# Gate and up projection in seven block products for each pair, value products of two heads on both column halves

## The chip, the cores and the metric

The kernel runs on one core of a Trainium2 chip. Its time is in device microseconds, the median of several executions. One more execution is recorded by the hardware profiler; the rows below are from it. Engines: TensorE (PE) multiplies, with its weight loads listed apart as PEld; VectorE (DVE), ScalarE (ACT) and GpSimd (POOL) do elementwise work; SyncE (SP) issues the DMAs.

## The reference

512 tokens of width 1024 pass a first block (a state-space scan, spatial gating, a mixture of experts) and then two layers of a second block. A layer has three attention branches, an output projection, and a dense feed-forward with 2816 hidden features. What the change touches, cut to its core:

```python
# neighbourhood attention, 8 heads of 64, per query block
sc = einsum('bnqhd,banchd->bhnqac', qb, kb) * scale + bias
p = softmax(where(col_valid, sc, -inf))
o = einsum('bhnqac,banchd->bnqhd', p, vb)
...
# differential attention, 4 heads, two score maps each
o = a1 - lam * a2
...
# dense feed-forward
gu = einsum('bsd,df->bsf', x, w_ffn_in[l])
hidden = silu(gu[..., :D_FF]) * gu[..., D_FF:]
ffn = einsum('bsf,fd->bsd', hidden, w_ffn_out[l])
x = layer_norm(DN_ALPHA * x + ffn, ln2_g[l], ln2_b[l])
```

## The kernel before

Every large product is done in three matmuls. An f32 operand `a` is split into a rounded part `ah` (a cast on ScalarE, L106) and the rest `al = a - ah` (a subtraction on VectorE, L107); `mm3` (L115 to L117) adds `ah*bh`, `al*bh` and `ah*bl` in PSUM. Weights come from memory in chunks of 128 x 1024 (`load_w`), are split into `whi` and `wlo` (three buffers each) and used.

A layer runs `mla`, `diff`, `na` (the three attention branches), `w_out2` (output projection, layer norm, transposition of the tokens into `xTh` and `xTl`) and `ffn`. In `ffn`, the hidden features come in 22 pairs of blocks of 128: `pg` is the gate block, `pu` the up block, each 8 chunks of the width times three matmuls of 512 tokens. The first two pairs work on column halves of 256 tokens, so that they can start when half of the tokens are there. Then come silu (L1688), the product (L1689) and the split of the hidden block into `hh` and `hl` (L1692, L1693), which all stay in SBUF. The down projection goes over the output in two halves `q`, over the 22 hidden blocks in 11 steps `i` of two, and over four token tiles `t`, each with its own PSUM tile.

In `na`, for a pair of heads `m` and two query blocks `i`, scores are 64 rows deep (L115 to L117 with `nqh`, `nkh`, heads on rows 0-63 and 64-127). After the softmax and a transposition (L1618) the value products (L1625) write both heads to PSUM rows 0-63, at different columns. In `diff`, two score maps of 64 rows each are computed one after the other.

PSUM has four tiles tagged `mm` and four tagged `aux`. The code is written in the order of the mathematics, but a scheduler places the instructions of each engine by its own estimate of time, so the order on an engine is not the written one. SyncE's loads go in order as buffers come free.

Of the kernel before, what the change touches and what calls it, by code (L numbers as in the profile page):

```python
# [17 lines left out]
NT = 4  # L18
# [19 lines left out]
class Net:  # L38
# [51 lines left out]
    def mm(self):  # L90
        return self.ps.tile([128, 512], F32, name="mm", tag="mm", bufs=4)
# [1365 lines left out]
    def diff(self, l):  # L1457
# [102 lines left out]
    def na(self, l):  # L1560
# [30 lines left out]
        for j in range(4):  # L1591
# [2 lines left out]
            gw = self.gate_w(0, l, 1)  # L1594
            for np_ in range(2):
                po = self.aux()
                for m in range(2):
                    r = slice(64 * m, 64 * m + 64)
                    hc = slice((2 * j + m) * 64, (2 * j + m + 1) * 64)
                    bt = at.tile([128, 512], F32, name="nb", tag="nb", bufs=4)  # L1600
                    nc.sync.dma_start(bt, self.a["na_bias"][l, j, np_, m])
                    ps = self.mm()
                    for i in range(2):
                        n = 2 * np_ + i
                        qs, ks = slice(n * 128, (n + 1) * 128), slice(kb[n], kb[n] + 256)
                        self.mm3(ps[:, i * 256:(i + 1) * 256], qh[r, qs], ql[r, qs], kh[r, ks], kl[r, ks], True, True)
# [14 lines left out]
                    for i in range(2):  # L1621
                        n = 2 * np_ + i
                        T, i0 = (VP, kb[n] // 128) if kb[n] % 128 == 0 else (VSH, kb[n] // 128)
                        for ii in range(2):
                            nc.tensor.matmul(po[0:64, m * 256 + i * 128:m * 256 + i * 128 + 128], T[:, i0 + ii, hc], PT[:, (2 * i + ii) * 128:(2 * i + ii + 1) * 128], start=ii == 0, stop=ii == 1)  # L1625
                    if np_ == 0 and m == 1 and j < 3:
                        nxt = prep(j + 1)
                src = [po[0:64, m * 256:(m + 1) * 256].rearrange("p (g r c) -> p g r c", g=4, r=8) for m in range(2)]
                dst = lambda x, m: perm(x[j][64 * m:64 * m + 64])[:, 4 * np_:4 * np_ + 4]
                for m in range(2):  # L1630
                    nc.scalar.copy(dst(oh, m), src[m])
                for m in range(2):
                    V.tensor_tensor(dst(ol, m), src[m], dst(oh, m).bitcast(F32), OP.subtract)
            self.gate(0, l, gw)
            for i in range(ng - 1):
                self.gate(0, l, self.gate_w(0, l))
# [11 lines left out]
    def w_out2(self, l):  # L1648
# [12 lines left out]
        for t in range(NT):  # L1661
# [6 lines left out]
                V.scalar_tensor_tensor(self.x[t][:, c], self.x[t][:, c], math.sqrt(2.0), p, op0=OP.mult, op1=OP.add)  # L1668
            self.layer_norm(self.x[t], LN_EPS, lg, lb)
            if t == 0:  # L1670
                self.new_xT()
            self.xT_block(self.x[t], t)
            self.dump("xa%d_%d" % (l, t), self.x[t])
        wo.release()

    def ffn(self, l):
        nc = self.nc
        V = nc.vector
        hp = self.pool("hid")
        tp = self.pool("hidt")  # L1680
        hh, hl = [], []
        for b in range(22):
            pg, pu = self.mm(), self.mm()
            outs = lambda p: [(p, slice(0, 256)), (p, slice(256, 512))] if b < 2 else [(p, ALL)]
            self.feat(self.a["w_f1"][l, b], self.xh, self.xl, outs(pg))
            self.feat(self.a["w_f1"][l, 22 + b], self.xh, self.xl, outs(pu))
            s = tp.tile([128, 512], F32, name="fs", tag="fs", bufs=3)
            nc.scalar.activation(s, pg, AF.Silu)  # L1688
            V.tensor_tensor(s, s, pu, OP.mult)  # L1689
            h = hp.tile([128, 512], F32R, name="hh%d" % b)  # L1690
            lo = hp.tile([128, 512], F32R, name="hl%d" % b)
            nc.scalar.copy(h, s)  # L1692
            V.tensor_tensor(lo, s, h.bitcast(F32), OP.subtract)  # L1693
            hh.append(h)
            hl.append(lo)
        lg, lb = self.bcast2(tp, "ln2_g", l), self.bcast2(tp, "ln2_b", l)

        ahead = 4
        st = [tp.tile([128, 2, 6], F32, name="fst%d" % t) for t in range(NT)]
        for q in range(2):  # L1700
            c = slice(q * 512, (q + 1) * 512)
            ps = [self.mm() for _ in range(NT)]
            last = 11 if q == 0 else 11 - ahead

            def mms(t, i, w):
                ts = slice(t * 128, (t + 1) * 128)
                for kk in range(2):
                    k, o = 2 * i + kk, slice(kk * 512, (kk + 1) * 512)
                    self.mm3(ps[t], hh[k][:, ts], hl[k][:, ts], w[0][:, o], w[1][:, o], k == 0, k == 21)

            for i in range(last):
                w = self.load_split(self.a["w_f2"][l, q, i], 1024)
                for t in range(NT):
                    mms(t, i, w)
            ws = []
            for i in range(last, 11):
                to = [tp.tile([128, 1024], F32R, name="fw" + n, tag="fw" + n, bufs=ahead - 3) for n in "hl"] if i < last + ahead - 3 else ()
                ws.append(self.split(self.load_w(self.a["w_f2"][l, q, i], 1024), 1024, *to))
# [177 lines left out]
```

## Time and profile before

| | us |
|---|---|
| median of 3 runs | 3253.01 (3251.31 to 3254.45) |
| the profiled execution | 3246.04 |
| its span | 3244.3 |
| PE busy | 3098.5 (96%) |
| VectorE busy | 2020.1 (62%) |
| ScalarE busy | 1453.4 (45%) |

The span runs from the first to the last instruction on the core; the profiled execution's time is 1.7 us more. Busy times of PE are sums in which overlapping matmuls count once. The first block fills the span to about 1302 us, the two layers the rest; layer 1's gate and up projection is the stretch from 2864 to 3112 us.

### The profile page before, as it was taken

The numbers are of one execution on the slowest core, as the hardware profiler recorded it, in microseconds if no ns is written. First come the engines' busy times: TensorE is split into PE (matmuls) and PEld (weight loads), VectorE is DVE, ScalarE is ACT, GpSimd is POOL, SyncE is SP. The second block draws the span as 40 slices with busy tenths as digits, with TensorE's granted clock in tenths as the row PEclk, the third lists the DMA queues.
The fourth block names the chain that finished last, engine by engine and source line by source line (L and its number), as shares of the span: only waits on it lengthen the run. The fifth ranks groups of instructions, "written<-read, shape, count | busy, mean of one in ns | idle before, by whom it ended". The sixth has DMA issues, their size and how long they took to land. (4 is left out here: it accounts for less than half of the span.)

```text
span 3244.3 us, 39811 instructions
## 1 busy us (share of the span) xinstructions
PE 3098.5 (96%) x14802; PEld 2447.2 (75%) x14802; DVE 2020.1 (62%) x3374; ACT 1453.4 (45%) x2455; POOL 378.1 (12%) x295
## 2 busy tenths in 40 slices
PE   7999999969999997899999999999999999999998
PEld 4887777746665654788777788888888777888887
DVE  7778765569888888676655653324675655653324
ACT  6544432347767775364544422221464534422221
POOL 1454200132121123000110000000000110000000
PEclk9999999979999999999999999999999999999999
DMA  5112245569999995112233322222312143422222
GB/s 194 53 43 76 93 152 180 181 255 405 342 349 353 366 355 199 67 57 75 69 119 119 113 89 98 91 98 88 107 59 80 59 146 98 135 67 97 91 98 78
DMA packets 140763, 469.82 MB, mean 145 GB/s; under 512 B 16268, under 2 KB 20364, under 8 KB 140568
## 3 DMA queue, kind: packets, MB, share of 16 engines
q1 hardware_dynamic: 139416, 463.08, 41.2%
q0 software_dynamic: 1152, 4.19, 0.3%
q8 instruction: 116, 1.90, 0.2%
q14 instruction: 79, 0.65, 0.1%
HBM read 456.71 MB, written 10.50 MB: 144 GB/s over the span
## 5 line engine op out<-in xcount | busy, mean ns | idle before, releaser
L107 DVE TENSOR_TENSOR wlo<-raw,whi 128x1024 fp32r<-128x1024 f32 (+4 forms) x384 | 434.0, 1133 | 515.7 <-ACT whi L106 514.5
L115 PE MATMUL mm<-xTh,whi 128*128 128x512 f32 (+2 forms) x1648 | 633.3, 385 | 6.1 <-ACT P L1233 2.6
L106 ACT CAST whi<-raw 128x1024 fp32r<-128x1024 f32 (+4 forms) x384 | 363.2, 948 | 603.0 <-PE mm L116 246.1
L116 PE MATMUL mm<-xTh,wlo 128*128 128x512 f32 (+2 forms) x1648 | 629.7, 383 | 0.0
L117 PE MATMUL mm<-xTl,whi 128*128 128x512 f32 (+2 forms) x1648 | 628.0, 382 | 0.7 <-POOL xTl L260 0.3
L115 PEld LDWEIGHTS mm<-xTh,whi 128*128 128x128 f32 (+1 forms) x1648 | 310.1, 188 | 75.7 <-ACT P L1233 4.2
L117 PEld LDWEIGHTS mm<-xTl,whi 128*128 128x128 f32 (+1 forms) x1648 | 309.7, 188 | 66.6 <-DVE xTl L260 1.5
L116 PEld LDWEIGHTS mm<-xTh,wlo 128*128 128x128 f32 (+1 forms) x1648 | 310.4, 188 | 62.9 <-issue 0.9
L115 PE MATMUL mm<-whi,xTh 128*128 128x512 f32 (+1 forms) x536 | 206.2, 386 | 2.5 <-DVE zt L555 2.1
L116 PE MATMUL mm<-whi,xTl 128*128 128x512 f32 (+1 forms) x536 | 205.8, 384 | 0.0
L117 PE MATMUL mm<-wlo,xTh 128*128 128x512 f32 (+1 forms) x536 | 203.0, 384 | 0.0
L1006 PE MATMUL mm<-wlo,XS 128*128 128x512 f32 x336 | 114.4, 412 | 18.3 <-DVE wlo L945 13.4
L116 PE MATMUL mm<-whi,hl 128*128 128x512 f32 x336 | 130.8, 389 | 0.0
L115 PE MATMUL mm<-whi,hh 128*128 128x512 f32 x336 | 130.4, 389 | 0.0
L117 PE MATMUL mm<-wlo,hh 128*128 128x512 f32 x336 | 129.7, 389 | 0.0
L1397 POOL TENSOR_TENSOR ql<-q,qh 128x512 fp32r<-128x512 f32 x16 | 20.6, 1290 | 885.0 <-ACT qh L1396 885.0
L115 PEld LDWEIGHTS mm<-whi,xTh 128*128 128x128 f32 x536 | 100.7, 188 | 23.0 <-DVE zt L555 2.5
L117 PEld LDWEIGHTS mm<-wlo,xTh 128*128 128x128 f32 x536 | 100.5, 188 | 19.6
L116 PEld LDWEIGHTS mm<-whi,xTl 128*128 128x128 f32 x536 | 100.7, 188 | 19.3
L945 DVE TENSOR_TENSOR wlo<-mraw,whi 128x1024 fp32r<-128x1024 f32 x82 | 108.7, 1341 | 8.9 <-ACT whi L943 8.6
L1005 PE MATMUL mm<-whi,XS 128*128 128x512 f32 x336 | 111.3, 405 | 1.6 <-ACT whi L943 1.6
L1689 DVE TENSOR_TENSOR fs<-fs,mm 128x512 f32<-128x512 f32 x44 | 30.3, 688 | 128.7 <-PE mm L117 128.7
(721 smaller groups left out, 6356.1 us busy)
## 6 DMA issues: line engine op xcount, KB each, us to landing
raw<-w_f SPq DMA_DIRECT2D x132, 512.0 KB
raw<-w_gate SPq DMA_DIRECT2D x68, 512.0 KB
mraw<-w_gate SPq DMA_DIRECT2D x52, 512.0 KB
mraw<-w_down SPq DMA_DIRECT2D x49, 512.0 KB
araw<-ada SPq DMA_DIRECT2D x48, 512.0 KB
mraw<-w_up SPq DMA_DIRECT2D x43, 512.0 KB
PT<-w_up SPq DMA_DIRECT2D x30, 512.0 KB
rawx<-w_down SPq DMA_DIRECT2D x28, 512.0 KB
```

Of the source, the lines that this page charges most:

```text
L106: nc.scalar.copy(hi[:, :n], raw[:, :n])
L107: nc.vector.tensor_tensor(lo[:, :n], raw[:, :n], hi[:, :n].bitcast(F32), OP.subtract)
L115: mm(out, ah, bh, start=first, stop=False)
L116: mm(out, al, bh, start=False, stop=False)
L117: mm(out, ah, bl, start=False, stop=last)
L945: eng.tensor_tensor(lo, raw, hi.bitcast(F32), OP.subtract)
L1005: nc.tensor.matmul(pp[q], X[:, k], wh[:, c], start=k == 0, stop=False)
L1006: nc.tensor.matmul(pp[q], X[:, k], wl[:, c], start=False, stop=k == 7)
L1397: nc.gpsimd.tensor_tensor(ql, q, qh.bitcast(F32), OP.subtract)
L1689: V.tensor_tensor(s, s, pu, OP.mult)
```

## The change

In the gate and up projection, pairs 0 and 1 stay as they were. For each of the other 20 pairs the product is taken as two by two blocks: gate and up rows by two halves of the width, times two halves of the width by two halves of the tokens. Seven products of such blocks with sums and differences of blocks replace the eight (`prod`: four chunks, three matmuls of 256 tokens each, so 84 matmuls of 256 columns in the place of 48 of 512). The factors on the token side (`T1` to `T4`) are made once for each layer, those on the weight side (`s12`, `s34`) for each pair, and parts of the results are added on VectorE. The f32 tokens are kept as `xTf`, with a second copy out of PSUM for that.

The hidden blocks are kept in f32 (`hs0` to `hs13`, and eight in the space of `xTf`, `hsx`). They are split later, by `hidden`: blocks 0 to 5 into a ring of two buffers `hh`, `hl`, in each half of the output anew; blocks 6 to 21 into buffers of their own. In the first half, the four PSUM tiles come from both tags.

The scores of two heads are written interleaved (`mm3_rows`). The value products of the second head go to PSUM rows 64-127, and one copy and one subtraction on 128 rows follow in the place of two on 64. The program's DMA scratch area is set to 4096, which moves SBUF addresses.

```diff
+    def mm3_rows(self, jobs):
+        mm = self.nc.tensor.matmul
+        for i in range(3):
+            for out, ah, al, bh, bl in jobs:
+                mm(out, al if i == 1 else ah, bl if i == 2 else bh, start=i == 0, stop=i == 2)
...
-                    for m in range(2):
-                        s = self.mm()
-                        r = slice(64 * m, 64 * m + 64)
-                        self.mm3(s, qh[r, qs], ql[r, qs], kh[r], kl[r], True, True)
+                    half = [slice(64 * m, 64 * m + 64) for m in range(2)]
+                    ss = [self.mm() for _ in half]
+                    self.mm3_rows([(s, qh[r, qs], ql[r, qs], kh[r], kl[r]) for s, r in zip(ss, half)])
+                    for m, s in enumerate(ss):
...
+                for i in range(2):
+                    n = 2 * np_ + i
+                    qs, ks = slice(n * 128, (n + 1) * 128), slice(kb[n], kb[n] + 256)
+                    self.mm3_rows([(ps[:, i * 256:(i + 1) * 256], qh[r, qs], ql[r, qs], kh[r, ks], kl[r, ks]) for ps, r in zip(pss, half)])
...
-                            nc.tensor.matmul(po[0:64, m * 256 + i * 128:m * 256 + i * 128 + 128], T[:, i0 + ii, hc], PT[:, (2 * i + ii) * 128:(2 * i + ii + 1) * 128], start=ii == 0, stop=ii == 1)
...
+                        for m, r in enumerate(half):
+                            hc = slice((2 * j + m) * 64, (2 * j + m + 1) * 64)
+                            nc.tensor.matmul(po[r, i * 128:(i + 1) * 128], T[:, i0 + ii, hc], PTs[m][:, (2 * i + ii) * 128:(2 * i + ii + 1) * 128], start=ii == 0, stop=ii == 1)
...
+                src = po[:, 0:256].rearrange("p (g r c) -> p g r c", g=4, r=8)
+                dst = lambda x: perm(x[j])[:, 4 * np_:4 * np_ + 4]
+                nc.scalar.copy(dst(oh), src)
+                V.tensor_tensor(dst(ol), src, dst(oh).bitcast(F32), OP.subtract)
...
+    def factors(self, pool):
...
+        V.tensor_tensor(b11, b12, b11, OP.subtract)
+        put("T1", b11)
+        V.tensor_tensor(b12, b22, b12, OP.subtract)
+        V.tensor_tensor(b22, b22, b11, OP.subtract)
+        put("T2", b22)
+        put("T3", b12)
+        V.tensor_tensor(b21, b21, b22, OP.subtract)
+        put("T4", b21)
+
+    def prod(self, p, w, x, first):
+        mm = self.nc.tensor.matmul
+        p = p[:, 0:256]
+        for k in range(4):
+            c = slice(k * 128, (k + 1) * 128)
+            mm(p, w[0][:, c], x[0][:, k], start=first and k == 0, stop=False, skip_group_check=not first)
+            mm(p, w[1][:, c], x[0][:, k], start=False, stop=False, skip_group_check=not first)
+            mm(p, w[0][:, c], x[1][:, k], start=False, stop=k == 3, skip_group_check=not first)
...
+        def begin(b):
+            G = self.load_w(self.a["w_f1"][l, b], 1024)
+            U = tp.tile([128, 1024], F32, name="rawu", tag="rawu", bufs=2)
+            nc.sync.dma_start(U, self.a["w_f1"][l, 22 + b])
+            a1 = self.split(G, 1024)
+            P, Q = self.mm(), self.aux()
+            g = gate()
+            self.prod(P, half(a1, 0), f["B11"], True)
+            nc.scalar.copy(g[:, 0:256], P[:, 0:256])
+            self.prod(Q, half(a1, 1), f["B21"], True)
+            V.tensor_tensor(g[:, 0:256], g[:, 0:256], Q[:, 0:256], OP.add)
+            st[b] = [G, U, P, g]
+
+        def middle(b):
+            G, U, P, g = st[b]
...
+            V.tensor_tensor(s12[:, lo], U[:, lo], U[:, hi], OP.add)
+            V.tensor_tensor(s12[:, hi], s12[:, lo], G[:, lo], OP.subtract)
+            w12 = self.split(s12, 1024, *parts())
+            V.tensor_tensor(s34[:, lo], G[:, lo], U[:, lo], OP.subtract)
+            V.tensor_tensor(s34[:, hi], G[:, hi], s12[:, hi], OP.subtract)
+            w34 = self.split(s34, 1024, *parts())
+            a22 = [self.wp.tile([128, 1024], F32R, name="w" + n, tag="w" + n, bufs=3)[:, 0:512] for n in ("hi", "lo")]
+            self.split(U[:, hi], 512, *a22)
+            R = self.aux()
+            t = tp.tile([128, 512], F32, name="ft", tag="ft", bufs=1)
+            self.prod(R, half(w12, 0), f["T1"], True)
+            nc.scalar.copy(t[:, 0:256], R[:, 0:256])
+            self.prod(P, half(w12, 1), f["T2"], False)
+            nc.scalar.copy(g[:, 256:512], P[:, 0:256])
+            self.prod(R, half(w34, 1), f["B22"], False)
+            V.tensor_tensor(g[:, 256:512], g[:, 256:512], R[:, 0:256], OP.add)
+            self.prod(P, half(w34, 0), f["T3"], False)
+            nc.scalar.copy(t[:, 256:512], P[:, 0:256])
+            nc.scalar.activation(g, g, AF.Silu)
...
+        def end(b):
+            G, U, P, g, a22, t = st.pop(b)
+            self.prod(P, a22, f["T4"], False)
+            s = hid[b]
+            V.tensor_tensor(s[:, 0:256], g[:, 0:256], P[:, 0:256], OP.mult)
+            V.tensor_tensor(t[:, 0:256], t[:, 0:256], t[:, 256:512], OP.add)
+            V.tensor_tensor(s[:, 256:512], g[:, 256:512], t[:, 0:256], OP.mult)
+
+        direct()
+        begin(2)
+        begin(3)
+        self.factors(xs)
+        for b in range(2, 22):
+            middle(b)
+            if b + 2 < 22:
+                begin(b + 2)
+            end(b)
...
+        KEEP = 6
...
+        def hidden(k):
+            if k not in kept:
+                w = [hp.tile([128, 512], F32R, name="h" + i, tag="h" + i, bufs=2) if k < KEEP else tp.tile([128, 512], F32R, name="h%s%d" % (i, k)) for i in "hl"]
+                nc.scalar.copy(w[0], hid[k])
+                V.tensor_tensor(w[1], hid[k], w[0].bitcast(F32), OP.subtract)
+                kept[k] = w
+            return kept[k] if k >= KEEP else kept.pop(k)
...
-            ps = [self.mm() for _ in range(NT)]
+            ps = [(self.aux if q == 0 and t % 2 else self.mm)() for t in range(NT)]
...
-    nc = bacc.Bacc("TRN2", target_bir_lowering=False, num_devices=1)
+    nc = bacc.Bacc("TRN2", target_bir_lowering=False, num_devices=1, dynamic_dma_scratch_size=4096)
```

**Order on PE in a pair, layer 1.** Before, PE goes through the 24 matmuls of a gate block (`mm_25670`, weights `whi_25674`) and then the 24 of its up block:

```order
L115 MATMUL mm_25670<-xTh_23962,whi_25674 128x512 [waits Activation_49]
L116 MATMUL mm_25670<-xTh_23962,wlo_25675 128x512 [waits DVE_49]
L117 MATMUL mm_25670<-xTl_23963,whi_25674 128x512
...
L117 MATMUL mm_25670<-xTl_23963,whi_25674 128x512
L115 MATMUL mm_25671<-xTh_23962,whi_25704 128x512 [waits Activation_49]
L116 MATMUL mm_25671<-xTh_23962,wlo_25705 128x512 [waits DVE_49]
```

In the changed kernel, the first of the twelve matmuls of each product from one pair's T4 to the next pair's (`xBl` holds B11 and B21, `xBr` holds B22 and T4, which takes the place of B12; `fhi` is the high part of a weight sum; the `aux` tiles here are R, for T1 and B22, and Q, for B21):

```order
L1744 MATMUL mm_27190<-xBr_25210,whi_27373 128x256 [waits Activation_49]
...
L1744 MATMUL mm_27315<-xT2_25846,fhi_27488 128x256
...
L1744 MATMUL aux_27502<-xBr_25210,fhi_27494 128x256 [waits Activation_49]
...
L1744 MATMUL mm_27565<-xBl_25206,whi_27561 128x256
...
L1744 MATMUL mm_27315<-xT3_25845,fhi_27494 128x256 [waits Activation_49]
...
L1744 MATMUL aux_27566<-xBl_25206,whi_27561 128x256
...
L1744 MATMUL aux_27627<-xT1_25844,fhi_27613 128x256
...
L1744 MATMUL mm_27315<-xBr_25210,whi_27498 128x256 [waits Activation_49]
```

Two runs of 24 matmuls became seven runs of twelve, which belong to several pairs at a time: T4 of one pair (`mm_27190`), T2, B22, T3 and T4 of the next (`mm_27315`, `aux_27502`), T1 of the one after it (`aux_27627`), B11 and B21 of the third (`mm_27565`, `aux_27566`). Only T2 stands between one pair's T4 and the next pair's B22.

**Order on ScalarE from the gate and up to the down projection, layer 1.** Before, it splits the last hidden blocks between casts of weights:

```order
L1692 CAST hh20_25804<-fs_25801 128x512 [waits DVE_49]
L1688 ACTIVATE fs_25870<-mm_25808 128x512 [waits PE_49]
L106 CAST whi_25921<-raw_25919 128x1024 [waits DMAHW1_49,Activation_49]
L106 CAST whi_25951<-raw_25949 128x1024 [waits DMAHW2_49,PE_49,Activation_49]
L1692 CAST hh21_25873<-fs_25870 128x512 [waits DVE_49]
```

In the changed kernel (`hs2` to `hs5` go to the ring `hh`, the others to buffers of their own):

```order
L1854 CAST hh_28333<-hs2_25517 128x512 [waits PE_49]
L106 CAST whi_28381<-raw_28379 128x1024 [waits DMAHW0_49,PE_49]
L1854 CAST hh_28337<-hs3_25518 128x512 [waits PE_49]
L106 CAST whi_28419<-raw_28417 128x1024 [waits DMAHW1_49,PE_49]
L1854 CAST hh6_28409<-hs6_25521 128x512
...
L1854 CAST hh20_28675<-hsx_25529 128x512
L1854 CAST hh_28371<-hs4_25519 128x512 [waits PE_49,Activation_49]
L1854 CAST hh21_28679<-hsx_25529 128x512
L106 CAST whi_28457<-raw_28455 128x1024 [waits DMAHW2_49,PE_49]
L1854 CAST hh_28375<-hs5_25520 128x512 [waits DVE_49,PE_49]
```

The split of hidden block 4 stands behind those of blocks 6 to 20; VectorE's subtractions stand in the same order.

**Order on PE in the value products of neighbourhood attention, layer 0** (`nVp` and `nVs` are values, `nPT` the transposed weights of one head). Before, one head by itself:

```order
L117 MATMUL mm_15061<-xTl_10632,whi_14865 128x512
L1625 MATMUL aux_14869<-nPT_14920,nVp_14544 64x128 [waits Activation_49]
L1625 MATMUL aux_14869<-nPT_14920,nVp_14544 64x128
L1625 MATMUL aux_14869<-nPT_14920,nVs_14545 64x128 x2
L115 MATMUL mm_15061<-xTh_10631,whi_14865 128x512
```

In the changed kernel (L1637 is the value product, L124 a matmul of `mm3_rows`):

```order
L124 MATMUL mm_14997<-nkl_14768,nqh_14732 128x256
L124 MATMUL mm_15000<-nkl_14768,nqh_14732 128x256
L124 MATMUL mm_14997<-nkh_14767,nqh_14732 128x256
L1637 MATMUL aux_14865<-nPT_14912,nVp_14544 64x128 [waits Activation_49]
L1637 MATMUL aux_14865<-nPT_14897,nVp_14544 64x128
L1637 MATMUL aux_14865<-nPT_14912,nVp_14544 64x128
L1637 MATMUL aux_14865<-nPT_14897,nVs_14545 64x128
L1637 MATMUL aux_14865<-nPT_14912,nVs_14545 64x128
```

The two heads (`nPT_14897`, `nPT_14912`) now alternate, and the scores of two heads (`mm_14997`, `mm_15000`) do so above them.

## Rows read from the trace of the kernel before

**Rows 1.** The page, busy time: engine, us busy (share of span) xinstructions.

```profile
PE 3098.5 (96%) x14802; PEld 2447.2 (75%) x14802; DVE 2020.1 (62%) x3374; ACT 1453.4 (45%) x2455; POOL 378.1 (12%) x295
```

**Rows 2.** Windows: us; each engine's busy us (instructions); PE clock; DMA share; GB/s.

```profile
2700.00:2791.00 91.00, 91.00 (x507) 71.04 (x506) 44.76 (x93) 43.01 (x101) 0.00 (x0) 1.00 0.27 86
2864.00:3112.00 248.00, 247.76 (x1165) 204.16 (x1164) 87.67 (x105) 70.04 (x91) 0.00 (x0) 1.00 0.29 95
3112.00:3232.00 120.00, 120.00 (x531) 99.33 (x530) 43.54 (x70) 21.50 (x21) 0.00 (x0) 1.00 0.24 82
```

**Rows 3.** Lines by form, 2864 to 3112: busy us, mean ns, idle before.

```profile
L115 PE MATMUL mm<-xTh,whi 128*128 128x512 f32 x319 | 126.2, 396 | 0.0
L107 DVE TENSOR_TENSOR wlo<-raw,whi 128x1024 fp32r<-128x1024 f32 x43 | 52.6, 1225 | 93.2 <-ACT whi L106 93.2
```

**Rows 4.** PE timeline, pair of blocks: start us, us, line, operation.

```profile
2949.62 0.40 PE L115 MATMUL mm<-xTh,whi 128*128 128x512 f32 x1
...
2952.42 0.40 PE L115 MATMUL mm<-xTh,whi 128*128 128x512 f32 x1
```

**Rows 5.** PE timeline, direct blocks in column halves: columns as in rows 4.

```profile
2869.80 0.28 PE L117 MATMUL mm<-xTl,whi 128*128 128x256 f32 x1
...
2871.23 0.28 PE L117 MATMUL mm<-xTl,whi 128*128 128x256 f32 x1
```

**Rows 6.** ACT timeline, end of a pair: start us, us, line, operation [idle].

```profile
2956.16 1.05 ACT L106 CAST whi<-raw 128x1024 fp32r<-128x1024 f32 x1 [4.11 <-issue]
2957.11 0.62 ACT L1692 CAST hh<-fs 128x512 fp32r<-128x512 f32 x1
```

**Rows 7.** DVE timeline, the same stretch: columns as in rows 6.

```profile
2956.12 0.69 DVE L1689 TENSOR_TENSOR fs<-fs,mm 128x512 f32<-128x512 f32 x1 [2.81 <-PE mm L117]
2957.24 1.23 DVE L107 TENSOR_TENSOR wlo<-raw,whi 128x1024 fp32r<-128x1024 f32 x1 [0.44 <-ACT whi L106]
2958.39 0.69 DVE L1693 TENSOR_TENSOR hl<-fs,hh 128x512 fp32r<-128x512 f32 x1
```

**Rows 8.** Lines by form, whole span, operations on 256 PSUM columns.

```profile
L1528 ACT COPY os<-aux 128x256 f32<-128x256 f32 x16 | 6.0, 373 | 26.8 <-PE aux L117 26.8
L992 DVE TENSOR_TENSOR XS<-aux,XS 128x256 fp32r<-128x256 f32 x32 | 13.0, 418 | 6.0 <-ACT XS L991 5.7
```

**Rows 9.** Windows around a wait of PE: columns as in rows 2.

```profile
318.00:322.80 4.80, 0.48 (x2) 0.05 (x1) 4.80 (x5) 1.76 (x5) 2.71 (x2) 0.81 0.03 14
322.80:326.00 3.20, 3.13 (x12) 2.87 (x13) 0.52 (x1) 0.57 (x2) 0.00 (x0) 0.50 0.87 288
326.00:330.00 4.00, 3.13 (x11) 2.27 (x10) 1.57 (x3) 1.67 (x5) 1.04 (x1) 0.78 0.08 32
```

**Rows 10.** PE timeline, value products of one head, before another matmul.

```profile
2706.44 0.65 PE L1625 MATMUL aux<-nPT,nVp 128*64 128x128 f32 x4
2706.92 0.60 PE L1625 MATMUL aux<-nPT,nVs 128*64 128x128 f32 x4
```

**Rows 11.** PE timeline, two products into PSUM rows 0-63 and 64-127.

```profile
783.09 1.07 PE L1059 MATMUL aux<-posT,s 16*64 16x512 f32 x4
784.09 0.74 PE L1006 MATMUL mm<-mwlo,HS 128*128 128x512 f32 x2
```

**Rows 12.** PE timeline, two stretches of neighbourhood scores and what follows each.

```profile
2686.34 0.39 PE L117 MATMUL mm<-nkl,nqh 64*128 64x256 f32 x2
...
2687.02 0.50 PE L117 MATMUL mm<-xTl,whi 128*128 128x512 f32 x1
...
2722.30 0.38 PE L115 MATMUL mm<-nkh,nqh 64*128 64x256 f32 x1
...
2723.55 0.50 PE L115 MATMUL mm<-xTh,whi 128*128 128x512 f32 x1
```

**Rows 13.** Lines by form and one window: sums of the modulation, z stage.

```profile
L671 DVE SCALAR_TENSOR_TENSOR adacc<-araw,cs,adacc 128x1024 f32<-128x1024 f32 x32 | 41.1, 1284 | 29.4 <-DMA araw<-ada 18.6 <-DMA adacc<-ada_b 10.5
...
340.00:356.00 16.00, 16.00 (x70) 12.88 (x69) 15.65 (x35) 4.33 (x6) 6.32 (x3) 1.00 0.12 35
```

More of the change, by code (lines that the diff above doesn't have):

```diff
@@ L1670, in w_out2, with new_xf @@
             if t == 0:
-                self.new_xT()
-            self.xT_block(self.x[t], t)
+                self.new_xf()
+            self.xf_block(self.x[t], t)
             self.dump("xa%d_%d" % (l, t), self.x[t])
         wo.release()
+    def new_xf(self):
+        self.XF = self.xTp.tile([128, 8, 512], F32, name="xTf", tag="xTh", bufs=1)
+        BL = self.xTp.tile([128, 4, 4, 256], F32R, name="xBl", tag="xTl", bufs=1)
+        self.xb = self.pool("xb", side="right")
+        BR = self.xb.tile([128, 4, 4, 256], F32R, name="xBr")
+        pair = lambda t, i: (t[:, i], t[:, i + 1])
+        self.f = {"B11": pair(BL, 0), "B21": pair(BL, 2), "B12": pair(BR, 0), "B22": pair(BR, 2)}
@@ new lines, in xf_block @@
+    def xf_block(self, x, t):
+        nc = self.nc
+        ts = slice(t * 128, (t + 1) * 128)
+        tb = slice(t % 2 * 128, t % 2 * 128 + 128)
+        for q in range(2):
+            pt = self.aux()
+            for k in range(4):
+                o = (4 * q + k) * 128
+                nc.tensor.transpose(pt[:, k * 128:(k + 1) * 128], x[:, o:o + 128], self.ident)
+            p3 = pt.rearrange("p (k n) -> p k n", k=4)
+            h, lo = (i[:, :, tb] for i in self.f["B%d%d" % (q + 1, t // 2 + 1)])
+            nc.scalar.copy(h, p3)
+            nc.vector.tensor_tensor(lo, p3, h.bitcast(F32), OP.subtract)
+            nc.scalar.copy(self.XF[:, 4 * q:4 * q + 4, ts], p3)
@@ new lines, in factors, with put @@
+    def factors(self, pool):
+        nc = self.nc
+        V = nc.vector
+        X = self.XF
+        f = self.f
+        for n in ("T1", "T3", "T2"):
+            t = pool.tile([128, 2, 4, 256], F32R, name="x" + n)
+            f[n] = (t[:, 0], t[:, 1])
+        f["T4"] = f.pop("B12")
+        lo, hi = slice(0, 256), slice(256, 512)
+        b11, b12, b21, b22 = X[:, 0:4, lo], X[:, 0:4, hi], X[:, 4:8, lo], X[:, 4:8, hi]
+        def put(n, x):
+            h, l = f[n]
+            nc.scalar.copy(h, x)
+            V.tensor_tensor(l, x, h.bitcast(F32), OP.subtract)
+        V.tensor_tensor(b11, b12, b11, OP.subtract)
[6 more added lines that the diff above has]
+        put("T4", b21)
@@ new lines, in prod, with ffn_in, direct @@
+    def prod(self, p, w, x, first):
+        mm = self.nc.tensor.matmul
+        p = p[:, 0:256]
+        for k in range(4):
+            c = slice(k * 128, (k + 1) * 128)
+            mm(p, w[0][:, c], x[0][:, k], start=first and k == 0, stop=False, skip_group_check=not first)
+            mm(p, w[1][:, c], x[0][:, k], start=False, stop=False, skip_group_check=not first)
+            mm(p, w[0][:, c], x[1][:, k], start=False, stop=k == 3, skip_group_check=not first)
+    def ffn_in(self, l, hid, ready):
+        nc = self.nc
+        V = nc.vector
+        f = self.f
+        xs = self.pool("xs", side="right")
+        tp = self.pool("hidt")
+        half = lambda w, i: [t[:, 512 * i:512 * i + 512] for t in w]
+        parts = lambda: [tp.tile([128, 1024], F32R, name="f" + n, tag="f" + n, bufs=3) for n in ("hi", "lo")]
+        gate = lambda: tp.tile([128, 512], F32, name="fg", tag="fg", bufs=3)
+        st = {}
+        def direct():
+            ws, ps = [], []
+            for b in range(2):
+                for i in range(2):
+                    ws.append(self.split(self.load_w(self.a["w_f1"][l, 22 * i + b], 1024), 1024, *(parts() if b else ())))
+                    ps.append(self.mm())
+            for n in range(2):
+                ts = slice(256 * n, 256 * n + 256)
+                for w, p in zip(ws, ps):
+                    for k in range(8):
+                        c = slice(k * 128, (k + 1) * 128)
+                        xh, xl = f["B%d%d" % (k // 4 + 1, n + 1)]
+                        self.mm3(p[:, ts], w[0][:, c], w[1][:, c], xh[:, k % 4], xl[:, k % 4], k == 0, k == 7)
+            for b in range(2):
+                g = gate()
+                nc.scalar.activation(g, ps[2 * b], AF.Silu)
+                V.tensor_tensor(hid[b], g, ps[2 * b + 1], OP.mult)
+                ready(b)
+        def begin(b):
[4 more added lines that the diff above has]
+            P, Q = self.mm(), self.aux()
+            g = gate()
+            self.prod(P, half(a1, 0), f["B11"], True)
[5 more added lines that the diff above has]
+            G, U, P, g = st[b]
+            sums = lambda: tp.tile([128, 1024], F32, name="fs", tag="fs", bufs=2)
+            lo, hi = slice(0, 512), slice(512, 1024)
+            s12, s34 = sums(), sums()
+            V.tensor_tensor(s12[:, lo], U[:, lo], U[:, hi], OP.add)
[17 more added lines that the diff above has]
+            nc.scalar.activation(g, g, AF.Silu)
+            st[b] += [a22, t]
+        def end(b):
[14 more added lines that the diff above has]
+            end(b)
+        tp.release()
+        xs.release()
+        self.xb.release()
@@ L1679, in ffn, with ready @@
         hp = self.pool("hid")
[L1680 to L1695, printed above, removed]
+        hid = [hp.tile([128, 512], F32, name="hs%d" % b) for b in range(14)]
+        hx = self.xTp.tile([128, 8, 512], F32, name="hsx", tag="xTh", bufs=1)
+        hid += [hx[:, b] for b in range(8)]
+        KEEP = 6
+        kept = {}
+        def hidden(k):
[5 more added lines that the diff above has]
+            return kept[k] if k >= KEEP else kept.pop(k)
+        def ready(k):
+            kept[k] = hidden(k)
+        self.ffn_in(l, hid, ready)
+        tp = self.pool("hidu")
         lg, lb = self.bcast2(tp, "ln2_g", l), self.bcast2(tp, "ln2_b", l)
@@ L1708, in mms @@
                     k, o = 2 * i + kk, slice(kk * 512, (kk + 1) * 512)
[L1709 removed]
+                    h = w[2 + kk]
+                    self.mm3(ps[t], h[0][:, ts], h[1][:, ts], w[0][:, o], w[1][:, o], k == 0, k == 21)
+            rows = lambda i: (hidden(2 * i), hidden(2 * i + 1))
             for i in range(last):
[L1712 removed]
+                h = rows(i)
+                w = (*self.load_split(self.a["w_f2"][l, q, i], 1024), *h)
                 for t in range(NT):
@@ L1717, in ffn @@
                 to = [tp.tile([128, 1024], F32R, name="fw" + n, tag="fw" + n, bufs=ahead - 3) for n in "hl"] if i < last + ahead - 3 else ()
-                ws.append(self.split(self.load_w(self.a["w_f2"][l, q, i], 1024), 1024, *to))
+                ws.append((*self.split(self.load_w(self.a["w_f2"][l, q, i], 1024), 1024, *to), *rows(i)))
             for t in range(NT):
```

31 lines of the change are left out of this document (12 added, 19 removed).

## Prediction

> **What bounds the kernel now.** I read the page's busy times first: TensorE (PE) is busy 96% of the span, VectorE 62%, ScalarE 45% [rows 1]. Then the windows, stage by stage: PE is busy for all of the neighbourhood-attention window, 247.76 of 248 us of the second layer's gate and up projection, and 120 of 120 of its down projection; in the projection VectorE works 87.67 us, in the down projection 43.54 [rows 2]. Layer 0 has the same stages and I take them as equal. So a PE stream sets the time there, and whatever shortens it shortens the run until another engine becomes late. VectorE's splits of weights wait for ScalarE's casts for 93.2 us in the projection [rows 3]: VectorE has room, but it is a chain, not a stream.
>
> **What a matmul costs.** In a pair of today's blocks twelve 512-wide matmuls take 2949.62 to 2952.42, 0.2333 us each [rows 4]. Where the direct pairs work on column halves, twelve 256-wide ones take 2869.80 to 2871.23, 0.1192 each [rows 5]. The listed 0.40 and 0.28 overlap each other and aren't summed. The products of the change are 256 wide with the same operands' shapes, so rows 5 price them. The Trainium skill (TensorE: Matmul & The Clock Gate, Back-to-back issue gap) gives a sustained 81 ns at 128 columns and 131 at 512, so halving the columns would not halve a matmul. By a line between its two figures a 256-wide one is an estimated 0.75 of a 512-wide one; the trace disagrees, with 0.51.
>
> **Seven products for eight.** A pair was 48 x 0.2333 = 11.20 us; it becomes 84 x 0.1192 = 10.01. That is 1.19 us over 20 pairs in 2 layers: **-47.6**. Bounds: at exactly half of a 512-wide matmul 9.80 and -56; if the twelve rows are optimistic by 1%, -43.5.
>
> **The work around a pair.** VectorE now does, for each pair, three 1024-wide subtractions, one 512-wide one, four 512-wide sums and five 256-wide operations. Start to start a 1024-wide subtraction is 1.15 us (2957.24 to 2958.39) though listed as 1.23; a 512-wide one, listed at 0.69, I take as 0.61 by the same 0.08 [rows 7]. The 256-wide ones that read PSUM are 0.418 listed [rows 8], 0.34 in a row. That makes 3 x 1.15 + 5 x 0.61 + 5 x 0.34 = 8.2 us, or 9.2 by listed durations, against PE's 10.01: busy 82 to 92%, still not the bound. ScalarE does three 1024-wide casts, one 512-wide, four 256-wide copies and a silu: 3 x 0.95 + 2 x 0.52 + 4 x 0.27 = 5.0 us (0.95 from 2956.16 to 2957.11, 0.62 less 0.10 for 512 [rows 6], 0.373 less 0.10 for 256 [rows 8]).
> What matters is who stands behind whom. In the order of the changed kernel ScalarE's cast of a coming gate block waits for the buffer that T4's product frees, and behind that cast stands the copy (L1809) that empties R after T1, for which the product B22 waits. B22 follows T4 with only T2's twelve matmuls between, 1.43 us of cover. The last matmul of T4 ends 0.16 after the next one's start (0.28 listed less 0.12 [rows 5]); with 0.95 for the cast, 0.37 for the copy and about 0.1 for two hand-overs the copy is done after 1.58. So PE waits some 0.15 us a pair where that order is regular, which it is in about half of the pairs: 20 x 0.15 = **+3**. Bounds: nothing where the cover holds; if VectorE's 9.2 us also waits once for a cast in series (1.05 + 0.04 and as much again for the hand-overs), 10.9 us a pair, 0.9 above PE's, +36. I stay at the low end because thirteen operations have two pairs in flight to slip past each other.
> The transposes of the last token block come after 48 matmuls of the direct pairs instead of after about 72. PE gets there up to 24 x 0.1192 = 2.9 us earlier while the layer norm that they need ends when it did; today PE has some two thirds of that to spare, so I take 0.9 a layer: **+1.8** (0 to 5.8). The eight T subtractions and splits (8 x 1.15 = 9.2 us) lie under the 192 direct matmuls, 192 x 0.1192 = 22.9 us.
>
> **From the up to the down projection.** Today the last hidden block is split as soon as it is there. In the changed kernel hidden blocks 2 to 5 share two buffers, so 4 must wait until PE has used 2, and the scheduler puts the fifteen splits of blocks 6 to 20 ahead of it on ScalarE and VectorE. From the start T of PE's second step (blocks 2 and 3), VectorE does a weight split, a product, block 3's split, another weight split, fifteen splits and block 4's: 1.15 + 0.34 + 0.61 + 1.15 + 15 x 0.61 + 0.61 = 13.0, and about 1.1 of waiting for casts at its head: T + 14.1. PE needs 24 matmuls of 120/531 = 0.226 us [rows 2] and four more on the high half: T + 6.3. Behind that wait stands every later matmul. So **+7.8** for each layer, 15.6; block 5 (T + 16.4) then comes in time. It costs nothing if the scheduler's order leaves PE busy with other products, and some 10 if the casts also wait for weights. In the second half of the columns the re-splits cost about **+0.5** in all.
> A wait of this size also costs clock. Where PE sat idle in the scan (busy 0.48 of 4.80 us), the next 3.2 us ran at a granted 0.50, the lower level, 1.2 GHz, and the 4 us after at 0.78 [rows 9]: 1.6 + 0.9 = 2.5 us lost. With a single wait of over 5 us I take that twice, **+5** (0 to 7).
>
> **Value products on both column halves.** One head's eight records run four in 0.48 us (2706.44 to 2706.92 [rows 10]), 0.97 for a head and 1.94 for two, one after the other. Two products into PSUM rows 0-63 and 64-127 already stand in the kernel: four records of 512 columns from 783.09 to the next line's start at 784.09, 1.00 us [rows 11], where four in a row at four times 0.12 us would take 1.9. So the halves overlap, and two heads should cost 0.97. There are 16 such groups: **-15.5**. The Trainium skill (TensorEngine Tiling (Array Packing), Key Properties) has tiles run independently but a change of tiling mode drain the engine; a drain at entry is in the row already, since one head's products are column tiles too. Bounds: -2 (nothing overlaps, only copies go) to -16.
>
> **Scores.** Heads in row groups overlap already where the order alternates them: eight records of the neighbourhood scores from 2686.34 to 2687.02 take 0.68 us, 0.085 each, against twelve from 2722.30 to 2723.55 in 1.25, 0.104 each, where the heads alternate in half [rows 12]. Twelve that alternate throughout should take about 0.90; seven runs a layer make 14 x 0.35 = **-5** (-1 to -8). In the differential scores the written interleave is undone by the scheduler in about 22 of 32 blocks, so **-1**.
>
> **Addresses.** The smaller DMA scratch moves SBUF addresses, and eight of the 32 modulation sums (1.284 us each) come early, into a stretch where VectorE is busy 15.65 of 16 us [rows 13]. Four stand ahead of a weight split that PE waits for soon after: 4 x 1.2 = 4.8 us if it has nothing to spare, nothing if it has as much; I take **+2**. PE was full where they left, so nothing is given back there.
>
> **Sum.** -47.6 + 3 + 1.8 + 15.6 + 0.5 + 5 - 15.5 - 5 - 1 + 2 = -41.2 us. The profiled run took 3246.04 (span 3244.3) and gives 3204.8; the median of the runs is 3253.01, 7.0 above it, and I forecast **3212**.
>
> **Rivals.**
> - VectorE's chain sets the pair. For it: thirteen operations, 82 to 92% busy, each waiting for PE or ScalarE; against it: two pairs in flight. Each 0.1 us a pair costs 4 us; 0.25 to 0.85 us more gives 3222 to 3246. **It ends slower than before** from 1.03 us more a pair (41.2 / 40), that is 11.1 us from pair to pair; at 12 us, where each of the thirteen waits 0.2 us, it would be 3212 + 40 x 1.9 = 3288.
> - The column halves run one after the other: against it rows 11, but those have 16 rows of weights and these 128. 3212 + 13.5 = 3226.
> - The wait at the down projection is hidden or the order is better than my walk: 3212 - 20.6 = 3191.
> - A 256-wide matmul costs three quarters of a 512-wide one where weights change each time: 84 x 0.175 = 14.7 us a pair, 3212 + 40 x 4.7 = 3400. Rows 5 change weights each time too. The sustained figures of the Trainium skill's TensorE page are what would make it so.
>
> **How the numbers follow.** Forecast (3200 to 3222) 0.54, halves in series 0.12, wait hidden 0.10, chain with 0.25 to 0.85 us 0.13 (0.05 of it near the old time), chain beyond 0.10, the page's price 0.01. Slower and faster begin 0.2%, 6.5 us, from 3253, about what a measurement of this kernel tells from no change. Faster: 0.54 + 0.12 + 0.10 + 0.08 = 0.84; same 0.05; slower 0.11. The range 3190 to 3245 takes in the hidden wait, halves in series and most of the milder chain; the forecast's own is 3200 to 3222.
>
> **What would show it.** Pairs of the middle of the projection should be 10.0 to 10.3 us apart on PE, the stage some 24 us shorter; over 11.2 the chain rival holds. PE should stand still 6 to 9 us for a split of the hidden block 4, once a layer, with a granted clock of about half behind it. Sixteen value records should take about 1 us. I am wrong if pairs wait for VectorE inside, or if PE stays busy from one projection to the other.

## The result

The changed kernel takes 3216.99 us (3214.44 to 3221.74, 4 runs) against 3252.16 (3249.38 to 3254.45): a ratio of 0.9894, 95% interval [0.9877, 0.9911], 35 us less. That is 5 us above the forecast of 3212 and inside its range. The gain is well beyond the 0.2% (6.5 us) that a measurement can't tell; the 5 us are below it. The profiled execution took 3218.56 with a span of 3216.8, 27.5 less than before. The span of before, though, comes from an execution that was 6 us below its median, and that of the changed kernel from one 1.6 us above, so the stages below add up to 27.5 and the medians to 35.

The page's busy times of the changed kernel, beside [rows 1]:

```profile
PE 3053.1 (95%) x16242; PEld 2484.7 (77%) x16242; DVE 2255.6 (70%) x3786; ACT 1592.5 (50%) x2715; POOL 378.3 (12%) x295
```

TensorE lost 45 us of busy time, and the share of the span in which it is busy fell too: new waits took a part of the gain. The windows by stage show where (columns as in [rows 2]): neighbourhood attention of layer 1, the direct pairs, the pairs in seven products, the change to the down projection, and the rest of that.

```profile
2675.00:2803.00 128.00, 127.89 (x709) 99.79 (x709) 73.92 (x136) 60.85 (x133) 0.00 (x0) 1.00 0.34 107
2847.00:2875.00 28.00, 27.13 (x214) 26.22 (x213) 25.25 (x43) 13.95 (x18) 0.00 (x0) 1.00 0.29 95
2900.00:3080.00 180.00, 180.00 (x1501) 179.03 (x1500) 147.31 (x226) 99.46 (x161) 0.00 (x0) 1.00 0.32 100
3080.00:3100.00 20.00, 15.02 (x53) 11.43 (x52) 16.28 (x25) 13.14 (x23) 0.00 (x0) 0.74 0.41 132
3100.00:3204.00 104.00, 103.97 (x459) 85.71 (x458) 41.59 (x70) 20.53 (x22) 0.00 (x0) 1.00 0.23 76
```

In the third row PE is busy 180.00 of 180 us, without a wait, and VectorE 147 of 180, 82%. In PE's timeline nine starts of the product T1 follow each other at the same distance. The first and the last of them are 79.52 us apart; that is eight pairs, 9.94 each or 0.1183 a matmul:

```profile
2980.35 0.28 PE L1744 MATMUL aux<-xT,fhi 128*128 128x256 f32 x1
...
3059.87 0.28 PE L1744 MATMUL aux<-xT,fhi 128*128 128x256 f32 x1
```

In the fourth row of the windows PE stands still for 5 us and the clock is 0.74. The waits of PE, from 3080 to the end, are two:

```profile
PE mm L115 <- ACT hh L1854: 4.0, 1, 4.0
PE mm L116 <- DVE hl L1855: 1.0, 1, 1.0
```

The timeline of PE shows the same place. The first column is the start, and the bracket gives the wait and what ended it:

```profile
3086.21 0.39 PE L117 MATMUL aux<-wlo,hh 128*128 128x512 f32 x1
3090.60 0.80 PE L115 MATMUL mm<-whi,hh 128*128 128x512 f32 x1 [4.00 <-ACT hh L1854]
...
3093.66 0.79 PE L116 MATMUL mm<-whi,hl 128*128 128x512 f32 x1 [0.98 <-DVE hl L1855]
3094.25 0.63 PE L117 MATMUL mm<-wlo,hh 128*128 128x512 f32 x1
3094.67 0.63 PE L115 MATMUL mm<-whi,hh 128*128 128x512 f32 x1
```

Starts are 0.43 apart behind the wait and 0.23 before it. VectorE's timeline says what was late: fifteen splits in a row, eight from `hs` tiles and seven from `hsx`, and only then block 4's.

```profile
3083.89 4.90 DVE L1855 TENSOR_TENSOR hl<-hs,hh 128x512 fp32r<-128x512 f32 x8
3088.70 4.30 DVE L1855 TENSOR_TENSOR hl<-hsx,hh 128x512 fp32r<-128x512 f32 x7
3092.91 0.69 DVE L1855 TENSOR_TENSOR hl<-hs,hh 128x512 fp32r<-128x512 f32 x1
```

The clock of the three stretches (windows: wait, then the 19 matmuls, then the rest) is 0.87, 0.50 and 1.00:

```profile
3086.60:3090.60 4.00, 0.00 (x1) 0.00 (x1) 4.00 (x8) 4.00 (x9) 0.00 (x0) 0.87 0.72 261
3090.60:3099.80 9.20, 8.22 (x19) 5.94 (x20) 5.74 (x9) 2.55 (x4) 0.00 (x0) 0.50 0.18 57
3099.80:3104.00 4.20, 4.20 (x20) 3.48 (x19) 2.05 (x3) 1.57 (x2) 0.00 (x0) 1.00 0.00 0
```

The first block is where the forecast was far off. Its last idle stretch of PE ends at 1324.26 us, where it ended at 1307.15 before: 17.1 us late. Here is that place, before and then changed:

```profile
1307.15 0.47 PE L1134 MATMUL aux<-ident,h 128*128 128x128 f32 x1 [21.76 <-DVE h L1212]
```

```profile
1324.26 0.47 PE L1141 MATMUL aux<-ident,h 128*128 128x128 f32 x1 [21.80 <-DVE h L1219]
```

The waits of PE from 340 to 425 us begin with one for a weight split, and VectorE's timeline has what stood ahead of that split, modulation sums (L678), one of which waited for its own load:

```profile
PE mm L117 <- DVE wlo L107: 3.8, 1, 3.8
```

```profile
352.85 1.28 DVE L678 SCALAR_TENSOR_TENSOR adacc<-araw,cs,adacc 128x1024 f32<-128x1024 f32 x1
...
356.77 1.28 DVE L678 SCALAR_TENSOR_TENSOR adacc<-araw,cs,adacc 128x1024 f32<-128x1024 f32 x1 [1.52 <-DMA araw<-ada]
...
358.11 2.35 DVE L107 TENSOR_TENSOR wlo<-raw,whi 128x1024 fp32r<-128x1024 f32 x2
```

Two heads' value products run together on PE as forecast: sixteen records take 1.03 us from 2694.67 to the next matmul at 2695.70. Before, the eight records of one head took 1.01 by the same measure, from 2706.44 [rows 10] to the next matmul at 2707.45 (the first line here; the others are the changed kernel's). The 0.97 of the forecast was twice the distance between its two lines.

```profile
2707.45 0.50 PE L115 MATMUL mm<-xTh,whi 128*128 128x512 f32 x1
```

```profile
2694.67 0.66 PE L1637 MATMUL aux<-nPT,nVp 128*64 128x128 f32 x8
2695.16 0.61 PE L1637 MATMUL aux<-nPT,nVs 128*64 128x128 f32 x8
2695.70 0.50 PE L115 MATMUL mm<-xTh,whi 128*128 128x512 f32 x1
```

### The profile page after: what moved, and what is told of

It reads as the page before. It is cut to its first block, busy times and chain, and to the rows that moved or that the text cites. A ratio compares the mean times of both kernels' runs of the same rounds, so it can differ in the third digit from the quotient of the medians.

```text
span 3216.8 us, 43492 instructions
## 1 busy us (share of the span) xinstructions
PE 3053.1 (95%) x16242; PEld 2484.7 (77%) x16242; DVE 2255.6 (70%) x3786; ACT 1592.5 (50%) x2715; POOL 378.3 (12%) x295
## 5 line engine op out<-in xcount | busy, mean ns | idle before, releaser
L107 DVE TENSOR_TENSOR wlo<-raw,whi 128x1024 fp32r<-128x1024 f32 (+4 forms) x340 | 379.3, 1118 | 310.8 <-ACT whi L106 309.5
L115 PE MATMUL mm<-xTh,whi 128*128 128x512 f32 (+2 forms) x880 | 344.1, 391 | 4.8 <-ACT P L1240 2.6
L116 PE MATMUL mm<-xTh,wlo 128*128 128x512 f32 (+3 forms) x880 | 340.7, 388 | 0.0
L117 PE MATMUL mm<-xTl,whi 128*128 128x512 f32 (+2 forms) x880 | 338.8, 386 | 1.1 <-DVE xTl L267 0.6
L115 PEld LDWEIGHTS mm<-xTh,whi 128*128 128x128 f32 (+1 forms) x880 | 165.5, 188 | 45.5 <-ACT P L1240 4.2
L117 PEld LDWEIGHTS mm<-xTl,whi 128*128 128x128 f32 (+1 forms) x880 | 165.3, 188 | 38.1 <-DVE xTl L267 2.2
L116 PEld LDWEIGHTS mm<-xTh,wlo 128*128 128x128 f32 (+1 forms) x880 | 165.6, 188 | 34.3 <-issue 1.2
L115 PEld LDWEIGHTS mm<-whi,xTh 128*128 128x128 f32 x536 | 101.4, 189 | 27.5 <-DVE zt L562 4.3
L952 DVE TENSOR_TENSOR wlo<-mraw,whi 128x1024 fp32r<-128x1024 f32 x82 | 107.0, 1328 | 12.8 <-ACT whi L950 12.2
L950 ACT CAST whi<-mraw 128x1024 fp32r<-128x1024 f32 x96 | 97.6, 1048 | 26.3 <-PE mm L1012 22.9
L1240 ACT ACTIVATE P<-mm,smv 128x512 f32<-128x512 f32 x128 | 88.2, 691 | 31.7 <-DVE P L1528 16.0
L107 DVE TENSOR_TENSOR flo<-fs,fhi 128x1024 fp32r<-128x1024 f32 x80 | 97.7, 1221 | 5.7 <-ACT fhi L106 4.6
```

Source lines behind the costliest of these rows:

```text
L107: nc.vector.tensor_tensor(lo[:, :n], raw[:, :n], hi[:, :n].bitcast(F32), OP.subtract)
L950: nc.scalar.copy(hi, raw)
L952: eng.tensor_tensor(lo, raw, hi.bitcast(F32), OP.subtract)
L1240: nc.scalar.activation(P, s, AF.Exp, bias=v[:, 8 + i:9 + i], accum_out=v[:, 16 + i:17 + i])
```

## The experiments

### Only the scratch area: `scr`

The kernel before with one edit:

```diff
-    nc = bacc.Bacc("TRN2", target_bir_lowering=False, num_devices=1)
+    nc = bacc.Bacc("TRN2", target_bir_lowering=False, num_devices=1, dynamic_dma_scratch_size=4096)
```

> The kernel before with the DMA scratch area of 4096 and nothing else changed. Theory (the addresses cost the first block its order): the second block starts some 17 us later than before, as in the changed kernel (1324.26 against 1307.15), and the run is 3269 against 3252. Rival (the loss in the first block comes from elsewhere, or is spread of the runs): within 3 us of the kernel before.

Measured: 3262.34 us (3261.52 to 3264.11) against 3250.30, ratio 1.0038 [1.0025, 1.0051]: 12 us slower. In the profiled execution the second block starts at 1322.66, 15.5 us late, and the waits of PE from 340 to 425 us are the changed kernel's:

```profile
PE mm L117 <- DVE wlo L107: 3.7, 1, 3.7
```

The theory holds in its sign and place, with 12 of the 17 us by the medians: the 17 was the distance between two single executions (see `pad`). Not a line of the program's work differs.

### The first block's addresses given back: `pad`

```diff
+        self.pad = self.pool("pad")
+        self.pad.tile([128, 3072], F32, name="pad")
         self.c1 = self.pool("consts1")
...
         self.hp.release()
+        self.pad.release()
```

> The changed kernel with an unused tile of 12288 bytes a partition below the first block's tiles, given up when the first block ends, so that these have the addresses of before. Theory (addresses): the first block is as fast as before, 17 us come back, 3200. Rival (the order of the first block does not matter, the loss is elsewhere): 3217.

Measured: 3205.03 us (3198.68 to 3210.20), ratio 0.9853 [0.9839, 0.9868], 12 us less than the changed kernel. The order in the first block is row for row that of before, on PE, VectorE and ScalarE, and of PE's waits from 340 to 425 us one of 1.5 us is left:

```profile
PE aux L594 <- DVE sg L590: 1.5, 1, 1.5
```

Adding the cost to the kernel before and taking it away from the changed one both give 12 us. (The changed kernel was measured in a series whose kernel before had a median 1.9 us higher; with each compared to the kernel before in its own series, the second is 10.)

In the profiled execution of `pad` the second block starts at 1314.12:

```profile
1314.12 0.47 PE L1143 MATMUL aux<-ident,h 128*128 128x128 f32 x1 [22.86 <-DVE h L1222]
```

That is 10.1 us before the changed kernel and still 7.0 after the kernel before, in the same order. So this time differs between executions, and one pair of traces can't price it. Five of the traces have the first block in the order of before (`before`, `val`, `pr`, `na`, `pad`): the second block starts at 1305.8 to 1314.1, 1309.5 on average. The four with the moved addresses (`ring`, `q128`, `scr` and the changed kernel) have 1320.9 to 1324.3, 1322.3 on average. The two groups do not overlap, and the 12.8 us between them agree with the medians.

### Other blocks in the ring: `ring`

```diff
-        KEEP = 6
+        RING = (0, 1, 2, 3, 10, 11)
...
-                w = [hp.tile([128, 512], F32R, name="h" + i, tag="h" + i, bufs=2) if k < KEEP else tp.tile([128, 512], F32R, name="h%s%d" % (i, k)) for i in "hl"]
+                w = [hp.tile([128, 512], F32R, name="h" + i, tag="h" + i, bufs=2) if k in RING else tp.tile([128, 512], F32R, name="h%s%d" % (i, k)) for i in "hl"]
...
-            return kept[k] if k >= KEEP else kept.pop(k)
+            return kept.pop(k) if k in RING else kept[k]
```

> The changed kernel with another six hidden blocks in the ring of two buffers: 0, 1, 2, 3, 10 and 11 in the place of 0 to 5. Blocks 4 and 5 then have buffers of their own, and their splits come first on ScalarE. Theory (the split of block 4 behind fifteen others makes PE stand still 5.0 us and run 19 matmuls at half clock, 4 us more, in each layer): 18 us less, 3199. Rival (the clock falls anyway at this place, or another wait takes the place, for weights): 0 to 10 us less.

Measured: 3203.03 us (3199.74 to 3204.47), ratio 0.9853 [0.984, 0.9865], 14 us less than the changed kernel by the medians (12 with each compared to the kernel before in its own series). By the traces it is 17.2: from the last matmul with `woh` or `wol` to the last of the down projection layer 0 takes 345.3 us for 353.3, layer 1 344.5 for 353.7, so 8.0 and 9.3 less. The layers differ because the clock stayed low for longer in layer 1 (last section). At the place of the wait PE is now busy throughout, at full clock:

```profile
3075.00:3085.00 10.00, 10.00 (x45) 8.28 (x45) 10.00 (x18) 8.94 (x16) 0.00 (x0) 1.00 0.50 167
3085.00:3100.00 15.00, 15.00 (x68) 12.39 (x67) 5.90 (x7) 3.96 (x5) 0.00 (x0) 1.00 0.45 141
```

As many blocks go through the ring as before; only which ones changed, and with it the order of the splits. So both the wait and the half clock hang on that order, and no other wait took their place.

### Both: `pr`

> Both edits of the two kernels above. If they are independent, the sum: 35 us less than the changed kernel, 3182. If the waits of one hide in the other, less.

Measured: 3188.17 us (3183.14 to 3193.50), ratio 0.9812 [0.9798, 0.9826]: 62 us less than before and 29 less than the changed kernel, where 12 and 14 make 26. Within the spread of the runs the two add up, so neither hides the other, and this version beats both kernels.

### Neighbourhood attention alone: `na` and `val`

`na` is the kernel before with the changed kernel's `na` and `mm3_rows`. `val` is `na` with the scores head after head:

```diff
-                for i in range(2):
-                    n = 2 * np_ + i
-                    qs, ks = slice(n * 128, (n + 1) * 128), slice(kb[n], kb[n] + 256)
-                    self.mm3_rows([(ps[:, i * 256:(i + 1) * 256], qh[r, qs], ql[r, qs], kh[r, ks], kl[r, ks]) for ps, r in zip(pss, half)])
+                for ps, r in zip(pss, half):
+                    for i in range(2):
+                        n = 2 * np_ + i
+                        qs, ks = slice(n * 128, (n + 1) * 128), slice(kb[n], kb[n] + 256)
+                        self.mm3(ps[:, i * 256:(i + 1) * 256], qh[r, qs], ql[r, qs], kh[r, ks], kl[r, ks], True, True)
```

> The kernel before with the whole edit of neighbourhood attention (scores of two heads interleaved, value products on both column halves) and nothing else. The trace of the changed kernel gives the stage 6.7 us less a layer: 13 us less than before. Rival (in the changed kernel the moved addresses helped the stage): less than 8.

> As the kernel above, but the scores of the two heads one after the other as before, so only the value products and their copies are changed. If the interleaved scores gain the 5 us of the prediction, this is 5 us slower than the kernel above. If the extra breaks in the runs of scores eat the gain, as their sum in the trace says (9.74 us before, 9.84 after in layer 1), it is within 2 us of it.

Measured: `na` 3238.65 us (3230.83 to 3239.89), ratio 0.9956 [0.9942, 0.9969], 12 us less than before; `val` 3244.16 (3236.82 to 3246.82), ratio 0.9983 [0.9973, 0.9993], 6 us less. Summed start to start over the stage of one layer in the traces, the 96 score records take 9.8 us before, 9.8 in `na` and 11.8 in `val`; the 128 value records 16.0, 9.6 and 10.0. From the first score to the first matmul of the output projection the stage takes 134.8 us a layer before, 128.1 in the changed kernel, 128.1 in `na` and 131.1 in `val`. `na` has the addresses of before, so the 6.7 us a layer are the edit's and the rival is refuted. The value products make 6.4 of them, so the gain of `na` over before is theirs. The interleaved scores are worth 2 us a layer against `val`, but nothing against before, because the edit also breaks the runs of scores up: the 96 records stand in ten runs a layer before, in sixteen in `na` and in `val`. `val`, which has the breaks without the interleave, pays 2 us for them, and the interleave gives these 2 us back. `na` shows both: twelve scores together take 0.90 us, one by itself 0.32.

```profile
2692.89 0.39 PE L124 MATMUL mm<-nkh,nqh 64*128 64x256 f32 x2
...
2693.79 0.51 PE L115 MATMUL mm<-xTh,whi 128*128 128x512 f32 x1
...
2701.67 0.38 PE L124 MATMUL mm<-nkh,nqh 64*128 64x256 f32 x1
2701.99 0.66 PE L1627 MATMUL aux<-ident,nb 128*128 128x128 f32 x4
```

Neither expectation for `val` was right as put. It is 5.5 us slower than `na` by the medians, near the 5 of the first, but not because interleaving gained 5 over before: the scores cost 2 us a layer more in `val` than in the kernel before, which I had not thought of.

### Matmuls of 128 columns: `q128`

The changed kernel, the direct pairs in four slices of tokens:

```diff
-            for n in range(2):
-                ts = slice(256 * n, 256 * n + 256)
+            for n in range(4):
+                ts, tb = slice(128 * n, 128 * n + 128), slice(n % 2 * 128, n % 2 * 128 + 128)
...
-                        xh, xl = f["B%d%d" % (k // 4 + 1, n + 1)]
-                        self.mm3(p[:, ts], w[0][:, c], w[1][:, c], xh[:, k % 4], xl[:, k % 4], k == 0, k == 7)
+                        xh, xl = f["B%d%d" % (k // 4 + 1, n // 2 + 1)]
+                        self.mm3(p[:, ts], w[0][:, c], w[1][:, c], xh[:, k % 4, tb], xl[:, k % 4, tb], k == 0, k == 7)
```

> The changed kernel with the direct pairs in four slices of 128 tokens in the place of two of 256: 384 matmuls of 128 columns for 192 of 256, in each layer. If a matmul of 256 columns is held up by its weight load (PE's weight loads are busy 179 of 180 us in the pairs), one of 128 takes the same 0.12 us: 23 us more a layer, 3262. If columns set its time, 0.06 to 0.07: 0 to 4 us more in all.

Measured: 3255.26 us (3250.64 to 3259.93), 38 us more than the changed kernel, from the same work in twice as many matmuls, and so nearer to the first expectation (46) than to the second (0 to 4). A window that holds only matmuls of 128 columns:

```profile
1925.00:1950.00 25.00, 25.00 (x226) 25.00 (x226) 11.10 (x12) 6.11 (x7) 0.00 (x0) 1.00 0.07 22
```

Start to start they are 0.112 us apart (mean of 223), with the weight loads busy 25.00 of 25; at 256 columns it is 0.118, with the loads busy 179 of 180. Half the columns save 6%. Matmuls of 64 columns elsewhere in the kernel (`J`, in the experts) are 0.112 apart as well, the median of 512. So in this kernel a matmul on the whole array, with a weight load of its own, took some 0.11 us however few its columns, and 256 columns are just above that. It is not the number of matmuls that sets this: the value products on two column halves follow each other at 0.064 us (1.02 over 16). That it is the weight load fits its busy share of 25.00 of 25, but no run takes the loads away, so this cause is not shown.

## Why the prediction was right, and where it was not

- **Seven products**: -47.6 and +3 of waits were forecast; at 9.94 us a pair it is 1.26 x 40 = -50.4, and there is no wait (the two rows from which I took 0.1192 are rounded to 0.01 us, which can make this difference). VectorE's chain was not the bound: its busy share of 82% is the low end of the forecast, and the wait of B22 for the copy of R does not occur on PE in 2900 to 3080 us. (One bound of that rival does not add up as written: 9.2 and twice 1.09 make 11.4 us a pair, not 10.9, and +55, not +36. Nothing in the forecast rests on it.) The third window refutes the rival that VectorE sets the pair, and the 9.94 us the one in which a 256-wide matmul costs three quarters of a 512-wide one.
- **Start**: +1.8 forecast; PE waits 0.9 us for the last tokens' layer norm once a layer, as said.
- **Up to down projection**: 15.6 of waits and 5 of clock forecast, 20.6. `ring` takes 8.0 and 9.3 us away in the two layers, 17.2 by the traces, 14 by the medians. The split of block 4 came at T + 12.6 (T = 3080.97, the end at 3093.60), not T + 14.1, so the wait was 5.0 and not 7.8; the lower clock lasted for 19 matmuls in layer 1, 0.2 us each, about 4 and not 2.5, and for 11 in layer 0. So the sign that I had named, 6 to 9 us of standing still, was missed. The +0.5 for the re-splits can't be seen: the stage is accounted for without it. The place, the late split and what hangs on it were right. The Trainium skill (TensorE: Matmul & The Clock Gate, The HAM clock gate) has the clock fall to its lower level after a time without work; the windows above agree, 0.87 over the 4.0 us of wait and 0.50 behind it.
- **Value products**: -15.5 forecast; 2 x 6.4 = -12.8 by the traces, where the whole of `na` gains 12 by the medians. Sixteen records take 1.02 us where they run together, as in half of the groups. In the others the scheduler sends the first product alone and lets scores come between, and the group costs 1.38: 4 x 1.02 + 4 x 1.38 = 9.6 a layer. The rival of halves in series is refuted.
- **Scores**: -5 and -1 forecast, nothing measured (9.8 us a layer before and after; the differential scores 20.0 both times). This step failed: I took the best stretch of before as the new rule and did not see that the runs would be broken more often. The price of alternation was right: a run of twelve that alternates throughout takes 0.90 us, as forecast, and against `val` the interleave gains 2 us a layer, 4 of the 5. But such a run occurs once a layer; ten runs became sixteen, and by `val` against before these breaks cost the same 2 us, so the sum stays.
- **Addresses**: +2 forecast, +12 measured (17 between the two profiled spans, 12.8 between the averages under `pad`). This term was the most mis-sized. I priced one wait by the work in front of it, 4.8 us at most, and left out that a sum could itself wait for its load (1.52 us), that PE then runs at half clock (starts 0.43 apart from 359.98), and that the order of the rest changes too: the gating stage that follows begins 10.6 us late (420.63 for 410.06), and the rest is lost by the end of the experts. By the averages of the same nine traces 8.8 us are lost by the time at which PE's wait of 14.8 us near 700 us ends, and 4.0 after it, in the experts; the other 4.3 of the 17.1 are the spread between executions. Which waits make up the experts' 4.0 was not settled.

Stage by stage, in the spans: the first block +17.1, neighbourhood attention -6.7 in each layer, the feed-forward -16.3 and -14.9, together -27.5. In the feed-forward, 50.4 for the pairs less 17.2 at the change to the down projection and 1.8 at the start makes -31.4 of the -31.2. The mechanisms of the pairs, the value products and the late split were right. That 3212 came within 5 us is partly luck: the scores, the addresses and the value products were too good by 6, by 10 and by 3, and the pairs and the down projection too bad by 6 and by 3.

## What to carry to other kernels

A block product that saves an eighth of the columns saves about an eighth of the time (here 11.20 to 9.94 us a pair) only while a matmul of half the columns takes about half the time. Here that held down to 256 columns (0.118 us) and no further (0.112 at 128); the weight loads, the likely limit, were by then busy 179 of 180 us, so look at their busy share before cutting further. When late work is moved behind a ring of buffers, read the order of the engine that refills it: what is ready goes first, and the block that is needed next may stand last. A change of addresses alone can reorder a scheduled program far from the edit, so compare the whole order, not only the part that was changed, and price the difference from several traces, not from one pair.

## What was not expected of the hardware

In the changed kernel the clock stayed at half for 9.2 us after the wait of 4.0 us (0.50 over 19 matmuls that were busy for 8.22 of 9.20 us), longer than the 3.2 us of [rows 9]; a second wait of 0.98 us lies within. In layer 0, at the same place, after the same two waits and in the same order, it stayed at half for 6.0 us only:

```profile
2151.36:2157.40 6.04, 5.06 (x11) 3.56 (x12) 5.34 (x8) 1.94 (x3) 0.00 (x0) 0.50 0.07 11
2157.40:2160.00 2.60, 2.60 (x12) 2.10 (x12) 0.57 (x1) 0.62 (x1) 0.00 (x0) 0.94 0.48 183
```

So the same wait cost 1.3 us more in one layer than in the other (9.3 and 8.0 given back by `ring`). And a matmul of 128 columns took 0.112 us where one of 256 took 0.118.
